# Layer 1's feed-forward: 18 of 22 gate and up tiles as one 2x2 block matrix product with seven block products

## The chip, the cores and the metric

The kernel runs on one core of a Trainium2 chip. The metric is the device time of one execution in microseconds (us). PE is TensorE (matmuls), PEld its weight loads, DVE VectorE, ACT ScalarE, POOL GpSimd, SP the engine whose queue issues the DMAs.

## The reference, cut to what matters

The program is one inference step of a two-layer backbone over 640 tokens (512 of a sample, 128 of a prompt), 1024 channels wide. Each layer has a mixer and then a feed-forward with a hidden width of 2816, all in float32:

```
def _swiglu(h, w_gate, w_up, w_down):
    return (jax.nn.silu(h @ w_gate) * (h @ w_up)) @ w_down
...
        xp = xp + gtf_p * _swiglu(_modulate(_rmsnorm(xp, norm_ffn_g[layer]), shf_p, scf_p), *ffn)
        xs = xs + gtf_s * _swiglu(_modulate(_rmsnorm(xs, norm_ffn_g[layer]), shf_s, scf_s), *ffn)
```

`_rmsnorm` divides each token by its root mean square, `_modulate` is h*(1+scale)+shift with one scale and shift per channel for the sample and one for the prompt. Layer 1's feed-forward is the last stage; a final norm follows.

## The kernel before, in words

Activations lie with channels on the 128 partitions: x is 8 tiles k of 128 channels by T = 640 tokens. Every float32 product is made of three: an operand is split into a rounded high part and the rest (`split`, L185: ACT writes hi at L186, DVE writes lo = x - hi at L187), and hi*hi, hi*lo and lo*hi are accumulated. `gemm` (L280) does this for one tile of 128 output channels: for each k three pairs, each on two halves of the columns, so 48 matmuls for 8 tiles k (L290). The two halves lie in the two banks of one `acc` buffer, of which there are two (pool `mm`); a pool `pm` has four more single banks.

A weight tile comes by one 512 KB DMA on SP's queue into one of two buffers `wraw` (`raw_w`, L269), and is split into one of three buffers `whi` and `wlo` (`split_w`, L274). A tile is loaded as soon as both readers of the older one are done.

`ffn(1)` (L393) works in three parts of 8, 7 and 7 hidden tiles (`FF_PARTS`). For a hidden tile f it loads gate and up weights and runs two `gemm`s on the moving operand `xh`, `xl` with GH = 322 columns to a half: 640 tokens and 4 columns for the shift. The operand is x times the norm's gain, but not yet divided by the root mean square, so that the matmuls can begin ahead of the norm's end; `scaled` (L365) multiplies the result by `rext`, the reciprocal root mean square of each token (DVE, L366). Then come SiLU (ACT, L413), the product with up (DVE, L414) and a split into `hh`, `hl`. After each part the 8 down tiles m run on it (320 columns to a half) and `residual` (L370) adds each into x with three DVE operations (L381). In the last part `ffn_end` (L432) takes the down product in two passes of 384 and 256 columns (L453), adds (L458), squares (L460), and writes the final norm (L470). Its weight tiles m = 3 to 7 are kept in buffers `wd` for the second pass.

The order on each engine is made by a scheduler ahead of time; on the chip each engine runs its list in order and waits at semaphores. The 12 arena buffers (`blk`) and the pools above limit how far it can run ahead.

## Time and profile before

| | |
|---|---|
| three runs of the kernel | 1951.6 us median, 1950.04 to 1951.79 |
| the profiled execution | 1948.95 us |
| its span in the profile | 1947.2 us |
| mean granted TensorE clock | 0.983 of 2.4 GHz |
| PE busy | 1865.1 us |
| DVE busy | 1242.4 us |
| ACT busy | 751.4 us |
| DMA queues' load | 34.4% of 16 engines' span |

The page lists one profiled execution. Busy time is the time in which an engine has an instruction in work; matmuls overlap in the pipeline, so one matmul's duration is longer than the distance to the next, and it is the distance that adds up. Some matmul records can be missing. "Idle before" a row is the time that its engine stood still ahead of it, and the name behind it is what ended that.

### The profile page before, as it was taken

Reading aid. Unit: us, or ns where it says so; the run is one execution under the profiler, and the core shown is the slowest. Engines: PE = TensorE matmul, PEld = TensorE weight load, DVE = VectorE, ACT = ScalarE, POOL = GpSimd, SP = SyncE. Lnnn points to the kernel's source line nnn. Section 1 sums busy time; section 2 is a strip of 40 time slices with the busy share of each in tenths; the row PEclk is TensorE's granted clock in tenths of the full one; section 3 lists DMA queues with packets and bytes.
Section 4 is the critical chain, followed back from the end, with each engine's and each line's share of the span. In section 5 each row is a group of like instructions: output and inputs, shape, how many; then the busy total and the mean of one; then the engine's idle time right before and its main releaser. Section 6 shows DMA issues by size and latency. Waiting matters only on the chain.

```text
span 1947.2 us, 30947 instructions
## 1 busy us (share of the span) xinstructions
PE 1865.1 (96%) x12556; PEld 1738.2 (89%) x12556; DVE 1242.4 (64%) x2041; ACT 751.4 (39%) x1246; POOL 369.4 (19%) x425
## 2 busy tenths in 40 slices
PE   4898999899999999999999999997999999999998
PEld 1886778899999999999988788865999999999997
DVE  7779933668837847876787786969464433433444
ACT  5453344532212212234654665664433221221222
POOL 1038800010000000012034533357341000000002
PEclk8999999999999999999999999999999999999999
DMA  7465355525524534432221222133422222222222
GB/s 289 117 154 175 120 164 129 205 98 174 166 75 150 162 110 148 141 105 89 80 77 55 75 63 92 50 107 92 162 67 76 76 69 75 75 69 84 76 59 83
DMA packets 100991, 215.82 MB, mean 111 GB/s; under 512 B 14944, under 2 KB 50416, under 8 KB 100336
## 3 DMA queue, kind: packets, MB, share of 16 engines
q1 hardware_dynamic: 100816, 213.83, 34.4%
q8 instruction: 99, 1.62, 0.3%
q14 instruction: 44, 0.36, 0.1%
q0 software_dynamic: 32, 0.02, 0.0%
HBM read 192.31 MB, written 18.84 MB: 108 GB/s over the span
## 4 chain that ended last, share of the span: by engine, by line
PE 83%; DVE 3%; ACT 1%; DMA 1%; issue 1%; DVEq 0%; SPq 0%; ACTq 0%
PE acc L290 71%; PE pm L453 1%; PE acc L453 1%; PE pm L627 1%; PE pm L709 1%; PE pm L1094 1%; PE pm L694 1%; DVE ssdw L683 1%; PE acc L1275 1%; PE pm L676 1%; DVE cv L560 1%; DMA ssq<-yd 1%; PE pm L713 1%; PE pm L226 1%; PE pm L1262 0%
## 5 line engine op out<-in xcount | busy, mean ns | idle before, releaser
L290 PE MATMUL acc<-xh,whi 128*128 128x322 f32 (+2 forms) x2320 | 548.3, 316 | 7.2 <-ACT xh L1169 6.2
L290 PE MATMUL acc<-xl,whi 128*128 128x322 f32 (+2 forms) x2320 | 547.8, 315 | 0.0
L290 PE MATMUL acc<-xh,wlo 128*128 128x322 f32 (+2 forms) x2320 | 546.5, 315 | 0.0
L186 ACT ACTIVATE whi<-wraw 128x1024 fp32r<-128x1024 f32 (+2 forms) x212 | 221.1, 1044 | 657.4 <-PE acc L290 416.3
L290 PEld LDWEIGHTS acc<-xh,whi 128*128 128x128 f32 (+1 forms) x2320 | 392.2, 190 | 23.1 <-issue 14.4
L290 PEld LDWEIGHTS acc<-xh,wlo 128*128 128x128 f32 (+1 forms) x2320 | 392.8, 189 | 11.1 <-issue 10.6
L290 PEld LDWEIGHTS acc<-xl,whi 128*128 128x128 f32 (+1 forms) x2320 | 393.6, 189 | 8.4 <-issue 7.9
L182 POOL TENSOR_TENSOR ssq<-ssq 128x640 f32<-128x640 f32 (+2 forms) x45 | 71.6, 1590 | 1122.4 <-ACT ssq L460 453.7
L187 DVE TENSOR_TENSOR wlo<-wraw,whi 128x1024 fp32r<-128x1024 f32 (+2 forms) x212 | 263.3, 1242 | 27.6 <-ACT whi L186 26.5
L366 DVE TENSOR_TENSOR ffw<-acc,rext 128x644 f32<-128x644 f32 x88 | 72.9, 829 | 200.8 <-PE acc L290 197.0
L381 DVE SCALAR_TENSOR_TENSOR x<-acc,mod,x 128x320 f32<-128x320 f32 x144 | 54.5, 434 | 163.9 <-PE acc L290 163.9
L246 DVE CUSTOM_DVE_ANT_0 junk<-adar,cond 128x1024 bf16<-128x1024 f32 x112 | 136.8, 1221 | 1.8
L290 PE MATMUL acc<-hh,wlo 128*128 128x320 f32 x592 | 134.5, 309 | 0.0
L290 PE MATMUL acc<-hl,whi 128*128 128x320 f32 x592 | 134.4, 308 | 0.0
L290 PE MATMUL acc<-hh,whi 128*128 128x320 f32 x592 | 134.2, 309 | 0.0
L560 DVE SCALAR_TENSOR_TENSOR cv<-cv,vecs 128x644 f32<-128x644 f32 x96 | 97.9, 1020 | 15.4 <-ACT cv L558 13.8
L290 PEld LDWEIGHTS acc<-hl,whi 128*128 128x128 f32 x592 | 98.9, 188 | 0.0
L290 PEld LDWEIGHTS acc<-hh,wlo 128*128 128x128 f32 x592 | 98.9, 188 | 0.0
L290 PEld LDWEIGHTS acc<-hh,whi 128*128 128x128 f32 x592 | 98.8, 188 | 0.0
L186 ACT ACTIVATE hh<-ffw 128x640 fp32r<-128x640 f32 x44 | 32.5, 739 | 95.4 <-DVE ffw L414 95.4
L683 DVE SCALAR_TENSOR_TENSOR ssdw<-ssdw,dtk,ssdcb 128x128 f32<-128x128 f32 x160 | 60.5, 442 | 11.3 <-ACT ssdw L681 11.0
L182 POOL TENSOR_TENSOR mt<-s5x,s5co 128x128 f32<-128x128 f32 x79 | 42.8, 550 | 119.4 <-ACT s5x L1034 114.5
(344 smaller groups left out, 2705.4 us busy)
## 6 DMA issues: line engine op xcount, KB each, us to landing
adar<-in_ada_w SPq DMA_DIRECT2D x56, 512.0 KB, 4.2
wraw<-in_ffn_w_gate SPq DMA_DIRECT2D x44, 512.0 KB, 3.3
wraw<-in_ffn_w_up SPq DMA_DIRECT2D x44, 512.0 KB, 3.3
wraw<-in_od_w_in SPq DMA_DIRECT2D x40, 512.0 KB, 3.3
wraw<-in_ffn_w_down SPq DMA_DIRECT2D x32, 448.0 KB, 3.3
wraw<-in_ev_w_in SPq DMA_DIRECT2D x16, 512.0 KB, 4.2
wraw<-in_ffn_w_down SPq DMA_DIRECT2D x16, 512.0 KB, 3.5
wraw<-in_od_w_out SPq DMA_DIRECT2D x16, 512.0 KB, 3.6
```

The lines of the kernel that those rows point to most:

```text
L182: e.tensor_tensor(o, a, b, op=op)
L186: self.nc.scalar.activation(hi, x, AF.Copy)
L187: self.nc.vector.tensor_tensor(lo, x, hi.bitcast(F32), op=OP.subtract)
L226: nc.tensor.matmul(ps[q:q + 32], self.condf[:, 2 * i + a], w[a][:, b * 512:b * 512 + 512], start=i == 0, stop=i == 3)
L246: nc.vector.tensor_tensor_reduce(out=junk, in0=w, in1=self.cond[:, s], scale=1.0, scalar=0.0, op0=OP.mult, op1=OP.add, accum_out=self.mod[ ...
L290: nc.tensor.matmul(ps[:mw, h, :n], a[:, k, :mw], b[:, h * n:(h + 1) * n], start=k0 + k == 0 and q == 0, stop=k0 + k == total - 1 and q == 2)
L366: self.nc.vector.tensor_tensor(t.rearrange("p (h n) -> p h n", h=2), ps[:, :, :GH], self.rext.rearrange("p (h n) -> p h n", h=2), op=OP.mult)
L381: nc.vector.scalar_tensor_tensor(xk[:, a:b], pv, gate[:, m, s:s + 1], xk[:, a:b], op0=OP.mult, op1=OP.add)
L453: nc.tensor.matmul(ps[:, :n], w[:, k], x[:, a:b], start=k == 0 and q == 0, stop=k == nf - 1 and q == 2)
L560: nc.vector.scalar_tensor_tensor(acc, cb[:, k:k + G], cw[:, k * 24 + wi:k * 24 + wi + 1], acc, op0=OP.mult, op1=OP.add)
L627: nc.tensor.matmul(ps, Bt[:, c], xw, start=True, stop=True)
L683: nc.vector.scalar_tensor_tensor(E[:, h], E[:, h], self.dt[:, 0, c, g * 8 + h:g * 8 + h + 1], cbs, op0=OP.mult, op1=OP.mult)
```

## The change

`build` calls `ffn_blocks(1)` instead of `ffn(1)`; layer 0 keeps `ffn`. The hidden tiles now come in parts of 4, 6, 6 and 6.

The first 4 tiles run as before. Beside them `token_forms` makes seven operands out of x: the 1024 channels are cut into two halves of 4 tiles k, the tokens into two halves of 320, and the four blocks b11, b12, b21, b22 (channel half, token half) are normalised, scaled and shifted first. The seven are b11, b21, b22, t1 = b12 - b11, t3 = b22 - b12, t2 = b22 - t1 and t4 = b21 - t2, each split into hi and lo (`fm`, seven arena buffers). One generator step, which makes all seven for one k, follows each of the 4 tiles.

For the other 18 tiles `block_pair` takes gate and up together as a 2x2 block matrix: a and b are the gate tile's two channel halves, c and d the up tile's. DVE makes s1 = c + d, s2 = s1 - a, s3 = a - c, s4 = b - s2 (`fws`). The seven products of 4 tiles k and 320 columns are a*b11, b*b21, s1*t1, s2*t2, s3*t3, s4*b22 and d*t4. Four of them accumulate in one bank X, which is read between them (by ACT for copies, by DVE for sums); one lies in the other bank A of the same `acc` buffer, two in a bank Y of `pm`. Nothing is multiplied by `rext` any more.

```diff
--- before.py
+++ after.py
@@ -428,6 +428,117 @@
                     after[1](m, self.xk(m))
             if last:
                 after[2]()
+
+
+    def token_forms(self, layer, xs):
+        nc = self.nc
+        fm = self.blks("fm", 7, [2, 4, TH], F32R)
+        self.forms = [(t[:, 0], t[:, 1]) for t in fm]
+        sh = self.mod[layer][:, 24:32]
+        for k in range(4):
+            for a, b, d in SEGS:
+                self.tt(nc.vector, xs[:, :, a:b], self.x[:, k::4, a:b], self.rext[:, None, d:d + b - a].to_broadcast([128, 2, b - a]), OP.mult)
+            for i in range(2):
+                for s, (a, b, d) in enumerate(SEGS):
+                    nc.scalar.activation(xs[:, i, a:b], xs[:, i, a:b], AF.Identity, scale=self.amul[:, 4 * i + k, s:s + 1],
+                                         bias=sh[:, 4 * i + k, s:s + 1])
+            b11, b12, b21, b22 = (xs[:, i, h * TH:h * TH + TH] for i in range(2) for h in range(2))
+
+            def put(n, x):
+                self.split(self.forms[n][0][:, k], self.forms[n][1][:, k], x)
+
+            sub = lambda o, x, y: self.tt(nc.vector, o, x, y, OP.subtract)
+            put(0, b11)
+            put(1, b21)
+            put(2, b22)
+            put(4, sub(b11, b12, b11))
+            put(6, sub(b12, b22, b12))
+            put(5, sub(b22, b22, b11))
+            put(3, sub(b21, b21, b22))
+            yield
+
+    def block_pair(self, layer, f, sc, ws, wd):
+        nc = self.nc
+        v = nc.vector
+        rg = self.raw_w(self.I["ffn_w_gate"][layer * NFF + f], 8)
+        ru = self.raw_w(self.I["ffn_w_up"][layer * NFF + f], 8)
+        a, b, c, d = (r[:, i * 4:i * 4 + 4] for r in (rg, ru) for i in range(2))
+        s1, s2, s3, s4 = (ws[:, i] for i in range(4))
+        ab = self.split_w(rg, 8)
+        self.tt(v, s1, c, d, OP.add)
+        self.tt(v, s2, s1, a, OP.subtract)
+        s12 = self.split_w(ws[:, 0:2].rearrange("p i k m -> p (i k) m"), 8)
+        self.tt(v, s3, a, c, OP.subtract)
+        self.tt(v, s4, b, s2, OP.subtract)
+        s34 = self.split_w(ws[:, 2:4].rearrange("p i k m -> p (i k) m"), 8)
+        self.split(wd[:, 0], wd[:, 1], d)
+        acc = self.mm.tile([128, 2, 512], F32, name="acc")
+        X, A, Y = acc[:, 0, :TH], acc[:, 1, :TH], self.psum()[:, :TH]
+
+        def product(ps, w, k0, form, first):
+            xh, xl = self.forms[form]
+            for k in range(4):
+                for q, (m, x) in enumerate(((w[0], xh), (w[0], xl), (w[1], xh))):
+                    nc.tensor.matmul(ps, m[:, k0 + k], x[:, k], start=first and k == 0 and q == 0, stop=k == 3 and q == 2, skip_group_check=not first)
+
+        p1, u2, p5, tu, tg, hd = sc
+        product(X, ab, 0, 0, True)
+        nc.scalar.activation(p1, X, AF.Copy)
+        product(A, ab, 4, 1, True)
+        self.tt(v, tg[:, :TH], A, p1, OP.add)
+        product(X, s12, 4, 5, False)
+        nc.scalar.activation(u2, X, AF.Copy)
+        product(Y, s12, 0, 4, True)
+        nc.scalar.activation(p5, Y, AF.Copy)
+        product(X, s34, 0, 6, False)
+        self.tt(v, tu, X, p5, OP.add)
+        product(Y, s34, 4, 2, False)
+        self.tt(v, tg[:, TH:], Y, u2, OP.add)
+        nc.scalar.activation(tg, tg, AF.Silu)
+        product(X, (wd[:, 0], wd[:, 1]), 0, 3, False)
+        self.tt(v, hd[:, TH:], tu, tg[:, TH:], OP.mult)
+        self.tt(v, hd[:, :TH], X, tg[:, :TH], OP.mult)
+        return hd
+
+    def ffn_blocks(self, layer):
+        nc = self.nc
+        gate = self.mod[layer][:, 40:48]
+        hb = self.big("hb", [2, 4, T], F32R)
+        wk = self.blk("ffw", [BLK])
+        forms = self.token_forms(layer, wk[:, 2 * G:2 * G + 2 * T].rearrange("p (i n) -> p i n", i=2))
+        ht = lambda k: (hb[:, 0, k], hb[:, 1, k])
+        for f0, f1 in ((0, 4), (4, 10), (10, 16), (16, NFF)):
+            nf = f1 - f0
+            if f0 == 4:
+                sb = self.blks("fsc", 2, [BLK])
+                ws = self.blk("fws", [4, 4, 128])
+                wd = self.blk("fwd", [2, 2, 4, 128], F32R)
+                h2 = self.blk("hc", [2, 2, T], F32R)
+                ht = lambda k: (hb[:, 0, k], hb[:, 1, k]) if k < 4 else (h2[:, 0, k - 4], h2[:, 1, k - 4])
+            for f in range(f0, f1):
+                if not f0:
+                    wg = self.load_w(self.I["ffn_w_gate"][layer * NFF + f], 8)
+                    pg = self.gemm(wg, self.xt, 8, GH)
+                    wu = self.load_w(self.I["ffn_w_up"][layer * NFF + f], 8)
+                    pu = self.gemm(wu, self.xt, 8, GH)
+                    tg = self.scaled(wk[:, :G], pg)
+                    hd = self.scaled(wk[:, G:2 * G], pu)
+                    for s, (a, b, d) in enumerate(SEGS):
+                        t, u = tg[:, d:d + b - a], hd[:, d:d + b - a]
+                        nc.scalar.activation(t, t, AF.Silu, bias=tg[:, NS + s:NS + s + 1])
+                        nc.vector.scalar_tensor_tensor(u, u, hd[:, NS + s:NS + s + 1], t, op0=OP.add, op1=OP.mult)
+                        self.split(*(h[:, a:b] for h in ht(f)), u)
+                    next(forms)
+                else:
+                    t = sb[f % 2]
+                    sc = [t[:, i * TH:i * TH + TH] for i in range(4)] + [t[:, 4 * TH:4 * TH + T], t[:, 4 * TH + T:4 * TH + 2 * T]]
+                    self.split(*ht(f - f0), self.block_pair(layer, f, sc, ws, wd[:, f % 2]))
+            if f1 == NFF:
+                self.ffn_end(layer, f0, nf, ht)
+                return
+            for m in range(8):
+                w = self.load_w(self.I["ffn_w_down"][layer * 8 + m][:, f0 * 128:f1 * 128], nf)
+                self.residual(self.xk(m), self.gemm(w, ht, nf, TH), m, gate)
 
     def ffn_end(self, layer, f0, nf, ht):
         nc = self.nc
@@ -1419,7 +1530,7 @@
             K.residual(K.xk(m), ps, m, gate, part[m // 4][:, m % 4])
             K.norm_tile(m, K.xk(m))
         K.norm_end()
-        K.ffn(1)
+        K.ffn_blocks(1)
 
 
 _OUTS = (("y", (128, 8, T)), ("cache", (2, 4, 128, 128)), ("s5", (2, 128, 32)), ("ssd", (2, 4, 128, 512)))
```

The scheduler puts the instructions of neighbouring tiles into one another. Three places show how. All of the program ahead of layer 1's feed-forward has the same order as before.

On DVE, in a tile's turn among the gate and up tiles before, a turn is these seven rows (the next gate's weights, the up product's scaling, the next up's weights, the product with SiLU, the split; `ffw` is the tile's work buffer):

```order
L366 TENSOR_TENSOR ffw_15209<-acc_15105,rext_83 128x644
L187 TENSOR_TENSOR wlo_15276<-wraw_15273,whi_15275 128x1024
L366 TENSOR_TENSOR ffw_15209<-acc_15160,rext_83 128x644
L187 TENSOR_TENSOR wlo_15340<-wraw_15337,whi_15339 128x1024
L414 SCALAR_TENSOR_TENSOR ffw_15209<-ffw_15209 128x512
L414 SCALAR_TENSOR_TENSOR ffw_15209<-ffw_15209 128x128
L187 TENSOR_TENSOR hl0_14978<-ffw_15209,hh0_14976 128x640
```

In the change a turn of a block tile has 14 rows; these are twelve of them, from the third block tile's time (14775 is the fourth tile's gate load, 14777 its up load; `fws` holds s1 to s4, `fsc0` and `fsc1` the scratch of even and odd tiles, `fwd` the split of d):

```order
L182 TENSOR_TENSOR fws_14415<-wraw_14777 128x512
L182 TENSOR_TENSOR fws_14415<-fws_14415,wraw_14775 128x512
L182 TENSOR_TENSOR fsc1_14414<-acc_14559,fsc1_14414 128x320
L182 TENSOR_TENSOR fsc1_14414<-fsc1_14414 128x320
L187 TENSOR_TENSOR wlo_14673<-fws_14415,whi_14672 128x1024
L182 TENSOR_TENSOR fws_14415<-wraw_14775,wraw_14777 128x512
L182 TENSOR_TENSOR fws_14415<-wraw_14775,fws_14415 128x512
L182 TENSOR_TENSOR fsc0_14413<-acc_14678,fsc0_14413 128x320
L187 TENSOR_TENSOR wlo_14780<-wraw_14775,whi_14779 128x1024
L182 TENSOR_TENSOR fsc1_14414<-acc_14559,fsc1_14414 128x320
L187 TENSOR_TENSOR fwd_14416<-wraw_14777,fwd_14416 128x512
L187 TENSOR_TENSOR hb_13556<-fsc1_14414,hb_13556 128x640
```

The turn's other two are the split of s1 and s2 (1024 columns) behind them and a 320-column sum of Y ahead of them. The fourth tile's weights are thus added up and split while the second tile's sums (`fsc1`) are finished.

On PE, in the same turn, at the end of the third block tile's first product (bank X of `acc_14678`), the queue goes on with the two matmuls of the third tile's s1*t1 (`fm4` is t1) in Y (`pm_14679`), and then with the second tile's s3*t3 in its own X (`acc_14559`):

```order
L482 MATMUL acc_14678<-fm0_13678,wlo_14661 128x320
L482 MATMUL pm_14679<-fm4_13682,whi_14666 128x320 x2
L482 MATMUL acc_14559<-fm6_13684,whi_14553 128x320 x2
L482 MATMUL acc_14559<-fm6_13684,wlo_14554 128x320
L482 MATMUL acc_14559<-fm6_13684,whi_14553 128x320 x2
L482 MATMUL acc_14559<-fm6_13684,wlo_14554 128x320
```

Nothing of the kind stood there before, where a tile's 48 matmuls of a product came in a row. In the whole turn the order is: third tile's b11, two matmuls of its t1, second tile's t3, the rest of t1, third tile's b21, second tile's t4, third tile's b22, third tile's t2, and the fourth tile's b11. At no place do two products of the same X follow each other.

On PE, at the seam between the fourth tile and the down tiles, the down tiles m = 0 (`acc_14147`) and m = 1 (`acc_14181`) first run over the hidden tiles 0 to 2, and then both over the hidden tile 3:

```order
L290 MATMUL acc_14181<-hb_13556,whi_14177 128x320 x4
L290 MATMUL acc_14181<-hb_13556,wlo_14178 128x320 x2
L290 MATMUL acc_14147<-hb_13556,whi_14143 128x320
L290 MATMUL acc_14181<-hb_13556,whi_14177 128x320
L290 MATMUL acc_14147<-hb_13556,whi_14143 128x320
L290 MATMUL acc_14181<-hb_13556,whi_14177 128x320
L290 MATMUL acc_14147<-hb_13556,whi_14143 128x320
L290 MATMUL acc_14181<-hb_13556,whi_14177 128x320
L290 MATMUL acc_14147<-hb_13556,whi_14143 128x320
L290 MATMUL acc_14147<-hb_13556,wlo_14144 128x320 x2
L290 MATMUL acc_14181<-hb_13556,whi_14177 128x320
L290 MATMUL acc_14181<-hb_13556,wlo_14178 128x320 x2
```

Before, at its first seam, m = 0 ran over seven of its eight hidden tiles before it needed the eighth.

## Rows read from the trace of the kernel before

**Rows 1.** The page: busy times, and the granted clock in 40 slices (tenths).

```profile
PE 1865.1 (96%) x12556; PEld 1738.2 (89%) x12556; DVE 1242.4 (64%) x2041; ACT 751.4 (39%) x1246; POOL 369.4 (19%) x425
PEclk8999999999999999999999999999999999999999
```

**Rows 2.** Chain that ended last, in order of time: start us, us, what.

```profile
1479.38 406.41 PE acc L290 x2748
```

**Rows 3.** Windows: us, busy by engine (count), PEclk, DMA share, GB/s.

```profile
1495.60:1580.80 85.20, 85.20 (x576) 85.20 (x575) 35.15 (x42) 23.04 (x31) 0.00 (x0) 1.00 0.24 75
1580.80:1637.00 56.20, 56.20 (x386) 56.20 (x385) 19.68 (x33) 9.23 (x10) 0.00 (x0) 1.00 0.24 76
1885.60:1936.50 50.90, 50.76 (x347) 50.26 (x345) 23.48 (x42) 14.66 (x24) 11.67 (x12) 1.00 0.22 68
1936.50:1947.20 10.70, 1.29 (x7) 0.81 (x6) 4.42 (x12) 0.68 (x2) 0.00 (x0) 0.61 0.29 99
```

**Rows 4.** Timeline of layer 1's feed-forward: start us, us, engine, line, operation, count.

```profile
1566.81 0.83 DVE L366 TENSOR_TENSOR ffw<-acc,rext 128x644 f32<-128x644 f32 x1 [5.05 <-PE acc L290]
...
1580.85 0.45 PE L290 MATMUL acc<-hh,whi 128*128 128x320 f32 x2
...
1581.05 0.83 DVE L366 TENSOR_TENSOR ffw<-acc,rext 128x644 f32<-128x644 f32 x1 [5.04 <-PE acc L290]
...
1585.54 0.45 PE L290 MATMUL acc<-hl,whi 128*128 128x320 f32 x2
...
1888.78 0.34 PE L453 MATMUL pm<-hh,whi 128*128 128x384 f32 x1
...
1891.76 0.34 PE L453 MATMUL pm<-hh,wlo 128*128 128x384 f32 x1
```

**Rows 5.** Groups by form from 1479.4 us on: count | busy, mean ns of one | idle before.

```profile
L187 DVE TENSOR_TENSOR wlo<-wraw,whi 128x1024 fp32r<-128x1024 f32 x48 | 58.7, 1223 | 0.9 <-ACT whi L186 0.3
L186 ACT ACTIVATE whi<-wraw 128x1024 fp32r<-128x1024 f32 x48 | 51.0, 1062 | 209.9 <-PE acc L290 124.0 <-issue 85.1 <-ACT rext L360 0.9
L366 DVE TENSOR_TENSOR ffw<-acc,rext 128x644 f32<-128x644 f32 x44 | 36.5, 829 | 165.5 <-PE acc L290 163.4 <-ACT rext L360 2.2
L187 DVE TENSOR_TENSOR hl<-ffw,hh 128x640 fp32r<-128x640 f32 x22 | 18.2, 826 | 17.7 <-ACT hh L186 17.7
L414 DVE SCALAR_TENSOR_TENSOR ffw<-ffw 128x512 f32<-128x512 f32 x22 | 16.4, 746 | 0.8 <-ACT ffw L413 0.8
L186 ACT ACTIVATE hh<-ffw 128x640 fp32r<-128x640 f32 x22 | 16.3, 739 | 46.8 <-DVE ffw L414 46.8
L414 DVE SCALAR_TENSOR_TENSOR ffw<-ffw 128x128 f32<-128x128 f32 x22 | 7.6, 346 | 0.0
L182 DVE TENSOR_TENSOR ssq<-ssq 128x384 f32<-128x384 f32 x1 | 0.6, 558 | 0.7 <-ACT ssq L460 0.7
L357 ACT ACTIVATE rext<-pm 128x512 f32<-128x512 f32 x1 | 0.6, 600 | 2.6 <-PE pm L356 2.6
L360 ACT ACTIVATE rext<-pm 128x128 f32<-128x128 f32 x1 | 0.3, 271 | 0.0
L290 PEld LDWEIGHTS acc<-hh,wlo 128*128 128x128 f32 x240 | 40.1, 188 | 0.0
```

**Rows 6.** Timeline of DVE: operations that follow each other without a wait.

```profile
1568.80 1.01 DVE L414 SCALAR_TENSOR_TENSOR ffw<-ffw 128x512 f32<-128x512 f32 x2
...
1602.14 1.14 DVE L381 SCALAR_TENSOR_TENSOR x<-acc,mod,x 128x320 f32<-128x320 f32 x3 [4.76 <-PE acc L290]
```

**Rows 7.** Timeline of DVE at the stage's start.

```profile
1480.10 0.83 DVE L366 TENSOR_TENSOR ffw<-acc,rext 128x644 f32<-128x644 f32 x1 [2.18 <-ACT rext L360]
```

**Rows 8.** DMA issues: count, KB each, median us from issue to landing.

```profile
adar<-in_ada_w SPq DMA_DIRECT2D x56, 512.0 KB, 4.2
wraw<-in_ffn_w_gate SPq DMA_DIRECT2D x44, 512.0 KB, 3.3
wglu<-in_s_w_glu SPq DMA_DIRECT2D x1, 1024.0 KB, 6.4
```

## The prediction

> **What bounds the kernel now.** The page comes first: PE is busy for 96% of the span, DVE for 64%, ACT for 39%, and the granted clock stands at nine tenths or more (2.4 GHz) from the second slice on [rows 1]. A share is an average, so the chain of waits comes next. There the changed stage is one piece: from 1479.38 us PE runs `gemm` after `gemm` for 406.41 us without another engine on the path [rows 2]. The windows say the same of its parts: among gate and up tiles and among down tiles PE has work for the whole window at a granted clock of 1.00, DVE for 41 and 35% of it [rows 3]. So here a matmul less is time less, as long as DVE, ACT and the weight loads keep up.
>
> **What a matmul costs.** From the scaling of one tile's up product (1566.81) to that of the next tile's (1581.05) lie 14.24 us and 96 matmuls of 322 columns [rows 4]: 148 ns each, 14.24 us a tile. From 1580.85 to 1585.54 there are 16 rows of two matmuls of 320 columns: 4.69/32 = 147 ns. In `gemm` two banks take turns; a block product puts 12 matmuls in a row into one bank. `ffn_end` does that too: 17 steps of 384 columns from 1888.78 to 1891.76 take 175 ns each [rows 4], by columns 146 ns for 320. One bank costs nothing extra; I take 146.6.
>
> **Removed and added on PE.** A block tile has 7 x 4 x 3 = 84 matmuls of 320 columns: 84 x 0.1466 = 12.31 us for 14.24, so 1.93 us less, 18 times 34.7 us. (By 146 ns it would be 35.4.) The down products keep their columns; 4, 6, 6 and 6 tiles make the same sum as 8, 7 and 7. The last 10.70 us stay [rows 3]. The page "TensorE: Matmul & The Clock Gate" of the Trainium skill, section "Back-to-back issue gap", gives N/2.4 + 2.5 ns between single matmuls. By it a tile would take 13.12 and a block tile 11.41 us, and the gain would be 30.8 us; the rows show 11 ns more per matmul, so the measured steps decide.
>
> **Added on DVE, block tiles.** Sizes that the trace lacks are read between neighbours: 512 columns 0.69 and 320 columns 0.49 us, from 384 at 0.558 and 640 at 0.826. A block tile has three splits of 1024 (1.223), one of 640 (0.826), four weight sums and one split of 512, five operations of 320: 3.67 + 0.83 + 3.46 + 2.46 = 10.4 us [rows 5]. Operations that adjoin take less than their durations add up to: 512 and 128 columns take 1.01 together, 1.09 apart [rows 6], so about 9.3 at best. ACT has three of 1.062, one of 0.6, three of 320 columns from PSUM (0.44, between 0.271 and 0.600) and two of 0.739: 6.6 us [rows 5]. Both lie below 12.31, but DVE now is 76 to 85% full, so its order counts.
>
> I walked one turn of the block stage by hand, in the order that the scheduler made, with these durations and 0.2 us from a product's last step to its reader (the next product starts at 1580.85, the scaling at 1581.05 [rows 4]). With PE never stopping, each wait ends in time. The tightest is the copy of X after s2*t2: ACT first splits s1 and s2 of the next tile, and ends 0.35 us before PE adds s3*t3. Next are DVE's read of X ahead of d*t4 (2 us to spare) and the free `acc` for the tile after (about 2 us). I allow 0.5 us for all 18 tiles; both ends are 0 and 0.35 for each, 6 us.
>
> **The weight loads.** There are two `wraw` for a gate and an up load, so up's next load starts only after DVE's split of d. From its landing to the next such split DVE has five operations of 512, four of 320 and two of 1024: 3.46 + 1.96 + 2.45 = 7.87 us. With 3.3 us from issue to landing [rows 8] the ring takes 11.2 us, and 12.1 with 4.2, the median beside other traffic: under 12.31, and hidden. SP's queue carries the same number of gate and up loads, and 32 instead of 24 down loads of fewer columns, in order.
>
> **Added in the first four tiles.** `token_forms` adds to DVE, per tile, two products with `rext` (1.23 and 0.42), four differences and seven splits of 320 (5.4): 13.2 us with the tile's own work, 11.5 when they adjoin, against 14.24 of PE. ACT gets four modulations and seven copies, some 5 us. PE's gate and up products need only that DVE scales each one in 7 us, which holds. But DVE starts at 1480.10, when the norm is done [rows 7], with PE already 13 us into the stage, and DVE's list has the fourth tile's forms ahead of its split.
>
> **The seams.** This is where I expect losses; before there were almost none.
> - Fourth tile to down. PE can run m = 0 and 1 over hidden tiles 0 to 2, 36 matmuls, 5.3 us. From the end of the up product DVE must scale it and do three splits of forms, a weight split, three differences and the product with SiLU before the hidden tile is split: with 0.2 us ahead 5.9 when they adjoin, and some 10 if DVE comes late to it. So 0.6 to 4.7 us; I take 1.5, nearer to the short one, because DVE has gaps to catch up. Then m = 0 and 1 end together and hold both `acc`, so m = 2 waits for `residual`, 1.14 us [rows 6]: 1.0.
> - Down to the first block tile. Both loads of the second block tile go out together, after s4 at 0.5 us, and land by 5.2 (4.7 lies between 3.3 for one load and 6.4 for 1024 KB [rows 8]); 4.6 us of DVE follow until its first weights are split, 9.8, where PE has come at 9.1: 0.7 (0 to 1.4). At the two later seams 0.4 in all.
> - Last block tile to down, twice: the down tile m = 1 needs the `acc` from which DVE still takes the last product: 0.2 + 0.49 us, then 0.3 for `residual`. 2.0 in all.
> - Into `ffn_end`: the same 0.7, and ACT squares m = 0 before it splits the weights of m = 3: 1.8. PE stood still for almost nothing there before [rows 3]. 2.5.
>
> The sum: -34.7 + 0.5 + 2.5 + 1.1 + 2.0 + 2.5 = -26.1 us. The profiled execution took 1948.95, so 1922.9; the median of the runs is 2.65 above it, and I predict **1925 us**. With no seam lost it would be 1951.6 - 34.7 = 1917; with each seam at its upper end (5.7 + 2 + 3 + 3.5) and 6 in the tiles some 1937. That is this case's own range, 1915 to 1937.
>
> **The rivals.**
> - *DVE becomes the bound* of the block tiles. For it: 76 to 85% busy, and DVE waits for ACT before each split; the split of a hidden tile waits 17.7/22 = 0.80 us today [rows 5]. Against it: the order puts other operations between ACT's half and DVE's. Were four of the five splits to wait 0.80, a turn would take 10.4 + 3.2 = 13.6, 18 x 1.3 = 23 us more: 1948. No change, or half of that.
> - *The weight ring is too slow*, and the kernel slower than before. If the gate and up loads hold each other up, as one transfer of 1024 KB at 6.4 us [rows 8], the ring takes 14.3, 18 x 2.0 = 35 us more: 1960. It begins to bind at 4.4 us from issue to landing and eats the gain at 5.9. Against it: the two go out over a microsecond apart, and the DMA engines are a quarter busy [rows 3].
> - *The bank X stops PE.* Were PE to wait at each of X's three returns until the reader is done, 2 x (0.2 + 0.44) + 0.2 + 0.49 = 2.0 us a tile and 35 in all would cancel the gain: 1961, slower. It decides if the product ahead of a return is X's own. The Trainium skill speaks against this part of the change: "Perfetto Trace Analysis", section "Matmuls", wants independent groups to rotate through banks so that the reading of one overlaps the next group. The built order sets other banks' products between, so I hold it unlikely; no row of before has such a return.
> - *A product costs more than its columns*: if a weight load (188 ns [rows 5]) were no longer hidden behind its matmul's neighbours and set the step, 84 x 0.188 = 15.8 us a tile, 63 us more: 1988. The single-bank rows at 175 ns speak against it.
>
> **How the numbers follow.** About 0.2%, 3.9 us, can be told from no change. The forecast's own case has 0.75. DVE as the bound 0.12, of which 0.08 still faster and 0.04 the same; the weight ring 0.07, of which 0.01 the same; the bank 0.04; dear products 0.02. Faster 0.83, same 0.05, slower 0.12. The range must leave out no more than 2 in 10: it goes from 1915 up to 1946, which takes in most of the DVE case and leaves out the three slow ones and the ends.
>
> **What would show it.** Right: in a window over the block tiles PE has work throughout, 12.3 us from one tile's first product to the next's; DVE is 75 to 85% busy; the product rows have steps of 146 to 147 ns; idle time of PE stands only at the four seams, 8 us in all, with `residual`, the hidden split and the weights `wd` as releasers. Wrong: a turn of 13 us or more, with PE waiting for a split (DVE is the bound), with DVE waiting for `wraw` (the ring), or for the copies of X; or PE waiting inside the first four tiles.

## The result and the profile after

The changed kernel takes **1921.95 us** (four runs, 1921.51 to 1923.59) where the kernel before took 1951.41 beside it: a ratio of 0.9852 (0.9835 to 0.9869), 29.5 us less. Predicted were 1925 us, 1915 to 1946. The profiled execution took 1922.12 us; the sum of the prediction, made against the profiled execution of before, gave 1922.9.

The page, to be held against [rows 1]: PE is as full as before with fewer matmuls, DVE goes from 64 to 70%.

```profile
PE 1837.2 (96%) x12340; PEld 1710.7 (89%) x12340; DVE 1342.8 (70%) x2255; ACT 818.7 (43%) x1374; POOL 369.6 (19%) x425
PEclk8899999999999999999999999999899999999999
```

Windows of the changed kernel, each over two turns of block tiles, one pair from each of the three parts (us, busy of PE, PEld, DVE, ACT, POOL with counts, PEclk, DMA share, GB/s; the counts take in instructions that a window's edges cut):

```profile
1581.58:1606.19 24.61, 24.61 (x170) 24.61 (x170) 19.60 (x29) 13.00 (x18) 0.00 (x0) 1.00 0.27 86
1699.04:1723.65 24.61, 24.61 (x170) 24.61 (x170) 18.57 (x27) 12.77 (x18) 0.00 (x0) 1.00 0.28 86
1816.35:1840.97 24.62, 24.62 (x171) 24.62 (x170) 19.54 (x29) 13.00 (x18) 0.00 (x0) 1.00 0.26 87
```

A turn is 12.305 us, 168 matmuls of 146.5 ns in two, at a granted clock of 1.00 (2.4 GHz), and PE has work for all of it. DVE is busy for 9.6 us of a turn and ACT for 6.5, on the average of the three windows. The tile before took 14.24 [rows 4].

PE's waits from the stage's start on, in the list by releaser (us in total, times, longest):

```profile
PE pm L344 <- DVE ssq L182: 1.8, 1, 1.8
PE pm L564 <- ACT wd L186: 1.3, 1, 1.3
PE acc L290 <- DVE fsc L182: 1.2, 2, 0.6
PE acc L290 <- DVE ffw L366: 0.9, 1, 0.9
PE acc L290 <- DVE x L381: 0.9, 1, 0.9
PE acc L564 <- DVE fsc L182: 0.7, 1, 0.7
PE pm L577 <- DVE rs L348: 0.6, 1, 0.6
```

The first and the last belong to the norm at the end and were there before (1.7 and 0.6, all that the same list of before has). No wait has a block product (L482) behind it: all stand at seams. A list counts only the idle time; what a seam costs is read in the timeline, as the distance between starts less the steps of 146.5 ns (148 for 322 columns, 175 for 384). PE at the start of the stage, at the third down tile, from a part's last block tile to the down tiles (the first of two such places), and at two places in `ffn_end`:

```profile
1481.63 0.46 PE L290 MATMUL acc<-xh,wlo 128*128 128x322 f32 x2
1482.98 0.54 PE L290 MATMUL acc<-xh,whi 128*128 128x322 f32 x2 [0.90 <-DVE ffw L366]
...
1532.54 0.46 PE L290 MATMUL acc<-hb,wlo 128*128 128x320 f32 x2
1533.87 0.38 PE L290 MATMUL acc<-hb,whi 128*128 128x320 f32 x1 [0.88 <-DVE x L381]
...
1631.53 1.92 PE L482 MATMUL acc<-fm,fwd 128*128 128x320 f32 x12
1634.03 0.86 PE L290 MATMUL acc<-hb,whi 128*128 128x320 f32 x4 [0.58 <-DVE fsc L182]
...
1867.12 1.93 PE L482 MATMUL acc<-fm,fwd 128*128 128x320 f32 x12
1869.73 0.59 PE L564 MATMUL acc<-hb,whi 128*128 128x384 f32 x2 [0.68 <-DVE fsc L182]
...
1873.83 0.34 PE L564 MATMUL acc<-hc,wlo 128*128 128x384 f32 x1
1875.47 0.62 PE L564 MATMUL pm<-hb,wd 128*128 128x384 f32 x2 [1.30 <-ACT wd L186]
```

Start of the stage 1.05 us; third down tile 1.04; last block tile to down 0.74, and 0.31 for `residual` at 1640.61, twice in all, 2.1; into `ffn_end` 0.85 + 1.47 and 0.5 lost in the next few steps, 2.8. That is 7.0 us; before the same places cost 0.3. So 34.7 - 6.7 = 28.0 us should be gone from the stage, and from its first matmul to the end of the span it went from 482.1 to 454.3 us, 27.8 less: the stage is accounted for to 0.2 us. The profiled executions differ by 26.8 us, because the stage began 0.9 us later in this one (1466.0 for 1465.1), with the same order ahead of it. The traces below, none with an edit ahead of the stage, begin it between 1464.3 and 1469.8, so that is no effect of the change. The medians differ by 29.5, because the median of before lies 2.5 us above its profiled execution and that of the change at its own.

The first wait is one that the prediction did not have. DVE at the stage's start, where [rows 7] had the scaling at once:

```profile
1480.87 1.23 DVE L182 TENSOR_TENSOR ffw<-x,rext 128x1024 f32<-128x1024 f32 x1 [2.01 <-ACT rext L357]
1482.02 0.82 DVE L366 TENSOR_TENSOR ffw<-acc,rext 128x644 f32<-128x644 f32 x1
```

`token_forms`' first product, x times `rext`, goes ahead of the scaling that frees `acc`.

### The profile page after: what moved, and what is told of

The parts are those of the page before. It is cut to its first block, busy times and chain, and to the rows that moved or that the text cites. A ratio compares the mean times of both kernels' runs of the same rounds, so it can differ in the third digit from the quotient of the medians.

```text
span 1920.3 us, 30941 instructions
## 1 busy us (share of the span) xinstructions
PE 1837.2 (96%) x12340; PEld 1710.7 (89%) x12340; DVE 1342.8 (70%) x2255; ACT 818.7 (43%) x1374; POOL 369.6 (19%) x425
## 4 chain that ended last, share of the span: by engine, by line
PE 82%; DVE 4%; ACT 1%; issue 1%; DMA 1%; DVEq 0%; SPq 0%; ACTq 0%
PE acc L290 59%; PE acc L482 8%; PE pm L482 3%; PE acc L564 1%; PE pm L738 1%; PE pm L564 1%; PE pm L820 1%; DVE ssdw L794 1%; PE pm L1205 1%; PE pm L805 1%; PE pm L787 1%; DVE cv L671 1%; PE acc L1386 1%; PE pm L824 1%; PE pm L226 1%
## 5 line engine op out<-in xcount | busy, mean ns | idle before, releaser
L290 PE MATMUL acc<-xh,whi 128*128 128x322 f32 (+1 forms) x1744 | 417.7, 319 | 8.4 <-ACT xh L1280 6.2
L290 PE MATMUL acc<-xl,whi 128*128 128x322 f32 (+1 forms) x1744 | 416.5, 317 | 0.0
L290 PE MATMUL acc<-xh,wlo 128*128 128x322 f32 (+1 forms) x1744 | 415.9, 317 | 0.0
L186 ACT ACTIVATE whi<-wraw 128x1024 fp32r<-128x1024 f32 (+3 forms) x202 | 204.0, 1011 | 489.1 <-PE acc L290 322.3
L290 PEld LDWEIGHTS acc<-xh,whi 128*128 128x128 f32 x1744 | 296.4, 190 | 24.6 <-issue 14.3
L290 PEld LDWEIGHTS acc<-xh,wlo 128*128 128x128 f32 x1744 | 296.2, 190 | 11.1 <-issue 10.6
L290 PEld LDWEIGHTS acc<-xl,whi 128*128 128x128 f32 x1744 | 297.5, 190 | 8.4 <-issue 7.9
L187 DVE TENSOR_TENSOR wlo<-wraw,whi 128x1024 fp32r<-128x1024 f32 (+3 forms) x202 | 242.6, 1202 | 33.0 <-ACT whi L186 32.5
L482 PE MATMUL acc<-fm,whi 128*128 128x320 f32 x576 | 127.5, 309 | 0.0
L482 PEld LDWEIGHTS acc<-fm,whi 128*128 128x128 f32 x576 | 96.2, 188 | 0.1
L482 PE MATMUL acc<-fm,wlo 128*128 128x320 f32 x288 | 88.8, 309 | 0.0
L794 DVE SCALAR_TENSOR_TENSOR ssdw<-ssdw,dtk,ssdcb 128x128 f32<-128x128 f32 x160 | 60.4, 441 | 11.2 <-ACT ssdw L792 11.0
```

The lines of the kernel that those rows point to most:

```text
L186: self.nc.scalar.activation(hi, x, AF.Copy)
L187: self.nc.vector.tensor_tensor(lo, x, hi.bitcast(F32), op=OP.subtract)
L290: nc.tensor.matmul(ps[:mw, h, :n], a[:, k, :mw], b[:, h * n:(h + 1) * n], start=k0 + k == 0 and q == 0, stop=k0 + k == total - 1 and q == 2)
L482: nc.tensor.matmul(ps, m[:, k0 + k], x[:, k], start=first and k == 0 and q == 0, stop=k == 3 and q == 2, skip_group_check=not first)
L794: nc.vector.scalar_tensor_tensor(E[:, h], E[:, h], self.dt[:, 0, c, g * 8 + h:g * 8 + h + 1], cbs, op0=OP.mult, op1=OP.mult)
```

## The experiments

The theory: PE bounds the block tiles at 12.31 us a turn, DVE and the loads are hidden, and the rest of the 34.7 us is lost at the seams. The rivals: the gain comes from something else in the change; or DVE, the weight ring (the two `wraw` buffers, loaded and used in turn) or the bank X is nearer to the bound than it looks. Ratios are to the kernel before, run on the same chip; "over the changed kernel" is the difference of ratios times 1951.6. A sharper measure is "the stage" in each profiled execution, from the stage's first matmul to the end of the span: the two traces of the changed kernel differ by 0.2 us in it. The section ends with a table of it.

**What the other parts of the change do.**

```diff
-        for f0, f1 in FF_PARTS:
+        for f0, f1 in parts:
...
-        K.ffn(1)
+        K.ffn(1, parts=((0, 4), (4, 10), (10, 16), (16, 22)))
```

> The kernel before, with layer 1's 22 hidden tiles in parts of 4, 6, 6 and 6 instead of 8, 7 and 7, and nothing else of the change. If the whole gain comes from the 84 matmuls that stand for 96, the parts alone gain nothing: PE has the same 2112 + 768 + 288 matmuls by columns, and the time is that of before, 1950 to 1954 us (a seam more, at most about 2 us). Rival: the parts themselves bring some of the gain (an earlier first down product, a shorter last part), then 1945 or less.

Measured: 1.0014 (1.0004 to 1.0023), 2.7 us slower. Its list of waits has two that before did not have:

```profile
PE pm L453 <- ACT wd L186: 0.9, 1, 0.9
PE acc L290 <- DVE x L381: 0.7, 1, 0.7
```

With forms, buffers and parts, and plain tiles throughout (beyond the lines shown, the later tiles use `fsc` as scratch and number their hidden tiles from the part's start):

```diff
-                if not f0:
+                if True:
...
-                    next(forms)
+                    if not f0: next(forms)
```

> The change with its parts, its seven operands and their buffers, but with plain gate and up products for all 22 tiles: the operands are made beside the first four tiles and not used. It prices what the change adds outside the block tiles. In the changed kernel PE stood still for 1.1 us at the start of the stage (the first operand's product with rext goes ahead of the scaling that frees acc) and 1.1 us at the third down tile, so 1 to 3 us over the parts alone, some 1953 to 1955. Rival: making the operands costs more, because DVE then has 13.2 us of work for 14.24 of PE: 1958 or more, with PE waiting inside the first four tiles.

Measured: 1.0014 (1.0004 to 1.0023) again. The list has 0.9 us for `ffw` at the start and 0.9 for the third down tile, but 0.4 for `wd`, and nothing inside the first four tiles: the forms cost little more than the wait at the start, 1.1 us of stage over parts_alone. From this kernel to the changed one the ratio falls by 0.0162, 31.6 us (30.4 of stage), and only the 18 later tiles differ. The rival that the parts or the forms bring the gain falls: the block products bring all of it and pay for their seams.

**What bounds a turn next.** The last product of every block tile, d*t4, is left out:

```diff
-        product(X, (wd[:, 0], wd[:, 1]), 0, 3, False)
+        pass
```

> Each block tile leaves out its last product, d*t4 (the sum X is read without it); all the work of DVE, ACT and the loads stays. It asks what bounds a turn next, after PE. PE's turn is then 72 x 0.1465 = 10.55 us. If nothing else is near, 18 x 1.76 = 31.7 us less than the changed kernel: 1890. If DVE is next (10.4 us of single operations), about the same, 1890 to 1893. If the weight ring is next, the turn stops at the ring's own time: in the changed kernel's trace one went from an up load's issue at 1586.62 over its use to the next issue at 1598.68, 12.06 us, and if that is its shortest, the gain is 18 x 0.25 = 5 us: 1917; at the 11.2 us of the prediction it is 1902.

Measured: 0.9707 (0.9690 to 0.9724), 28.3 us under the changed kernel of 31.7. A product of 12 matmuls is worth nine tenths of its time, 1.57 us of 1.76. Most of the missing 3 us is inside the tiles now: in the list PE waits for ACT's copy of Y. SP's timeline has the up loads 11.6 and 12.6 us apart where PE's turn would be 10.55, and the chain of work that ended last shows how that reaches PE, from the load over ACT's splits to the product in Y:

```profile
PE pm L482 <- ACT fsc L492: 3.1, 10, 0.5
```

```profile
1576.15 1.06 SPq L271 DMA_DIRECT2D wraw<-in_ffn_w_up  x1
...
1588.78 0.33 SPq L271 DMA_DIRECT2D wraw<-in_ffn_w_up  x1
...
1600.38 0.33 SPq L271 DMA_DIRECT2D wraw<-in_ffn_w_up  x1
```

```profile
1588.78 4.14 DMA wraw<-in_ffn_w_up
1593.48 1.04 ACT whi L186
1594.53 0.74 ACT hb L186
1595.65 2.03 PE pm L482 x12
```

So the ring is next after PE, as the prediction's 11.2 to 12.1 said. Eighteen turns longer by 1.05 us would have lost 19; the up loads at the start of a part go out only 8.1 to 8.9 us apart, and I put it down to this lead that most of it is hidden over six tiles.

**How much DVE has left.** Four, and eight, more operations a tile that nobody reads:

```diff
-        self.tt(v, tu, X, p5, OP.add)
+        self.tt(v, tu, X, p5, OP.add); [self.tt(v, p1, tu, p5, OP.add) for _ in range(4)]
```

> Each block tile gets four more additions of 320 columns on DVE whose result nobody reads (0.49 us each alone, about 0.40 adjoining). If only DVE's sum of work counts, 10.4 + 1.6 to 2.0 = 12.0 to 12.4 us, 11 when operations adjoin, is still hidden under PE's 12.31: 1921 to 1924. If the weight ring has no slack, what stands between an up load's landing and the split of d grows by three of them or so, 1.2 to 1.5 us: 18 x 1.2 = 22 us more, less what the lead of one tile covers at the start of each part: 1935 to 1945.

> Eight more additions of 320 columns on DVE in each block tile instead of four. In a window of 49 us (four turns) DVE was busy 38.84 us in the changed kernel and 43.65 with four more, 1.2 us a turn for four; with eight a turn has 9.75 + 2.4 = 12.15 us of DVE, just under PE's 12.31. If the sum alone counts, still 1921 to 1926. If DVE cannot do without its waits for the up load and for ACT (1.3 us a turn with four more), a turn takes some 13.3 us and 18 turns 18 us more, less the lead at the start of each part: 1932 to 1942, with PE waiting for wlo or fsc.

Measured: 0.9858 (0.9843 to 0.9874) with four, no change; 0.9878 (0.9854 to 0.9902) with eight, 5 us over the changed kernel. Its interval reaches into the changed kernel's, but its stage is 5.1 us longer too. The same window of 49 us (four turns) in the changed kernel, with four and with eight, one kernel to a fence:

```profile
1567.00:1616.00 49.00, 49.00 (x337) 49.00 (x336) 38.84 (x56) 26.06 (x37) 0.00 (x0) 1.00 0.26 81
```

```profile
1567.00:1616.00 49.00, 49.00 (x336) 49.00 (x335) 43.65 (x72) 25.58 (x37) 0.00 (x0) 1.00 0.22 74
```

```profile
1567.00:1616.00 49.00, 48.41 (x326) 47.56 (x326) 47.67 (x85) 24.39 (x35) 0.00 (x0) 1.00 0.24 80
```

With eight, DVE (the third busy time) is at 97% and sets the pace: d*t4 begins at 1594.18 and 1606.79, 12.61 us a turn for 12.31, and PE waits for it inside the block tiles:

```profile
PE acc L482 <- DVE fsc L182: 1.9, 5, 0.5
```

So almost all of DVE's idle time in the changed kernel, some 2.5 us a turn, is spare, and not a chain of waits that it needs. The DVE rival was further off than its chance of 0.12 made it.

**The bank X.** First each tile's products in the order of the code, which keeps the scheduler from setting two tiles into each other:

```diff
-            xh, xl = self.forms[form]
+            xh, xl = self.forms[form]; es = ExitStack(); es.enter_context(self.behind(nc.tensor))
...
+            es.close()
```

> PE takes a block tile's seven products in the order of the code, one tile after the other, instead of the scheduler's mixture of two tiles. Between two products of the same bank X then stands one product of another bank, 1.76 us. The reader of X needs 0.2 + 0.44 us (ACT copy) or 0.2 + 0.49 (DVE sum), so it ends in time unless its engine is in a long split (1.06 on ACT: 0.2 + 1.06 + 0.44 = 1.70). If one product between two returns is enough, no change against the changed kernel: 1920 to 1925 us. If the mixture of two tiles is what hides the readers, PE waits 0.3 to 1 us at several of the returns of each tile: 1930 or more.

> As tiles_in_order, but with s2*t2 directly behind a*b11, so that once in a tile X is written again with no other product between. The wait is then at least 0.2 + 0.44 us for the copy p1, and up to 1.7 where ACT is in a split: 18 x 0.64 = 11.5 us to 18 x 1.7 = 31 us over tiles_in_order, so 1933 to 1955. If returns to a bank cost nothing on PE (the copy is overlapped anyway), 1920 to 1925.

Measured: **1.0037** (1.0026 to 1.0048) in order, 36 us over the changed kernel, the whole gain and more; 0.9988 (0.9978 to 0.9997) with t2 directly behind a*b11, 27 us over it. Of the first expectation the slow case came, that the mixture hides the readers, but not at the places where it looked for the waits. The second failed in its sign: x_adjacent was to be 11.5 to 31 us slower than tiles_in_order and is 10 us faster; that its time lies in the range given for it is chance. The list of the first names two waits a tile:

```profile
PE acc L482 <- DVE fsc L182: 14.3, 18, 1.9
PE acc L482 <- ACT fsc L486: 12.3, 18, 0.7
```

and the timeline shows where they stand: between a*b11 and b*b21, and between b*b21 and s2*t2.

```profile
1587.71 0.31 PE L482 MATMUL acc<-fm,wlo 128*128 128x320 f32 x1
1588.73 0.56 PE L482 MATMUL acc<-fm,whi 128*128 128x320 f32 x2 [0.70 <-ACT fsc L486]
...
1590.45 0.31 PE L482 MATMUL acc<-fm,wlo 128*128 128x320 f32 x1
1591.41 0.56 PE L482 MATMUL acc<-fm,whi 128*128 128x320 f32 x2 [0.65 <-DVE fsc L182]
```

At 1588.73 the product of b21 begins, in bank A, and what it waited for is the copy of bank X. No data make it wait; X and A are the two banks of one `acc` buffer. If the waits go by the buffer, they end when A lies anywhere else; the order of the code stays as in tiles_in_order:

```diff
-        X, A, Y = acc[:, 0, :TH], acc[:, 1, :TH], self.psum()[:, :TH]
+        X, A, Y = acc[:, 0, :TH], self.psum()[:, :TH], self.psum()[:, :TH]
```

> As tiles_in_order, but the product b*b21 goes to a bank of pm instead of the second bank of X's acc buffer. In tiles_in_order PE waited for the copy p1 before that product, though it writes another bank, and for the sum that reads A before X was written again: 26.6 us by releaser, 36 us in the time. If PE's waits go by the whole acc buffer, taking A out of it ends both, because between two returns of X stands a product of 1.76 us and its reader needs 0.64 to 0.69: 1922 to 1928 us. If what counts is that only one product stands between the returns, the waits stay, at X's second and third return, and the time stays at 1945 or more.

Measured: 0.9844 (0.9828 to 0.9860), as fast as the changed kernel. Of the waits of a block product the list keeps one:

```profile
PE acc L482 <- ACT fsc L486: 0.4, 1, 0.4
```

In x_adjacent, too, the buffer was at work: there s2*t2, directly behind a*b11, waits for the first copy, p1 (L486), and b*b21 in bank A for the second, u2 (L488). Neither waits for DVE's sum, and the two waits add up to 19.5 us instead of 26.6, most of the difference between the two runs:

```profile
PE acc L482 <- ACT fsc L486: 10.0, 18, 0.7
PE acc L482 <- ACT fsc L488: 9.5, 18, 0.5
```

So one other product of 1.76 us between two returns of X is enough, and the 26.6 us of waits in tiles_in_order came from the shared buffer. In the changed kernel the same products share the buffer, and the mixture of two tiles hides the waits. In the stage in_order_a_apart is even 2.7 us shorter than the changed kernel; its list has none of the three waits for `fsc` at the seams. That the bank rival's price was met (35 us predicted, 36 measured) is luck: it counted three waits a tile, each ahead of a product in X for X's own reader, 0.64 to 0.69 us, and two others came, one ahead of A for X's reader and one ahead of X for A's. One of its steps is confirmed by x_adjacent: where the product ahead of a return is X's own, PE waits, 0.56 us each for 0.64.

**The weight ring.** Each up load waits for a load of half of it into the same buffer:

```diff
-        self.nc.sync.dma_start(raw[:, :nk, :mw], ...)
+        [self.nc.sync.dma_start(raw[:, :n, :mw], ...[:, :n]) for n in ([nk // 2] if more else []) + [nk]]
...
-        ru = self.raw_w(self.I["ffn_w_up"][layer * NFF + f], 8)
+        ru = self.raw_w(self.I["ffn_w_up"][layer * NFF + f], 8, more=True)
```

> Each up load of a block tile is preceded by a load of half of it into the same buffer, which it must wait for: from issue to landing some 2.5 us more than the 4.4 us of the changed kernel, about 6.9. It prices the rival of the weight ring. With six products the ring turned in 11.5 us with loads of 4.1 us, so it is 7.4 us and the load: 14.3 us a turn, 2.0 us over PE's 12.31, 18 x 2.0 = 36 us less the lead at the start of each of three parts (two turns' worth, some 4 us each): 1940 to 1950. If there is slack that the ring does not show, because DVE and ACT take the operations in another order when a load is late, under 1930.

Measured: 0.9917 (0.9902 to 0.9932), 13 us over the changed kernel, between the two cases expected. The chain of waits, from the first part (start us, us, what), follows the ring:

```profile
1577.10 2.58 DMA wraw<-in_ffn_w_up
1579.69 3.23 DMA wraw<-in_ffn_w_up
...
1589.14 3.32 DMA wraw<-in_ffn_w_up
1592.47 4.00 DMA wraw<-in_ffn_w_up
...
1602.76 3.42 DMA wraw<-in_ffn_w_up
```

The two loads together take 5.8 and 7.3 us; from the landing (1582.92, 1596.47) to the next issue DVE needs 6.2 and 6.3 us (6.7 to 7.1 in the later turns of the other two parts), not the 7.87 of the prediction nor the 7.4 of the expectation, because the scheduler sets nine operations there instead of the changed kernel's eleven. Turns of 12.0 and 13.6 follow, and of the rival's price a good third. In this order the ring would bind at 12.31 - 6.25 = 6.1 us from issue to landing in the first part, and at 5.2 to 5.6 in the others, rather than at 4.4. In the changed kernel's own order the eleven operations are those that the prediction counted: an up load that landed at 1578.8 is followed by the next issue at 1586.62, 7.8 us later. Its loads in the stretch from 1567 to 1616 us are at the limit of 4.4 already, without a wait of PE:

```profile
wraw<-in_ffn_w_up SPq DMA_DIRECT2D x3, 512.0 KB, 4.4
```

So the run prices a longer load in an order of its own. How much longer a load the changed kernel's order would bear is not shown.

**The seams mended.** One mend for each kind of wait: the first operands behind the first tile's scalings on DVE; the weights `wd` split ahead of the first square; odd down tiles in two banks of `pm` (`Two` puts two such banks in place of an `acc`).

```diff
+                    up = [i for i in nc.cur_bb.bb.instructions if i.engine == nc.vector.engine][-1]
...
-                    next(forms)
+                    with self.tc.issue_after(up):
+                        next(forms)
...
-                self.residual(self.xk(m), self.gemm(w, ht, nf, TH), m, gate)
+                ps = Two((self.psum(), self.psum())) if m % 2 else None
+                self.residual(self.xk(m), self.gemm(w, ht, nf, TH, ps=ps), m, gate)
...
-                if len(ws) == m:
+                while len(ws) < min(m + 5, 8):
...
-                nc.scalar.activation(sq if m else ssq, x, AF.Square)
+                with self.behind(nc.scalar):
+                    nc.scalar.activation(sq if m else ssq, x, AF.Square)
```

> The changed kernel with three mends, one for each kind of wait that its trace shows on PE. (1) The first operand's product with rext stands behind the first tile's two scalings on DVE: 1.1 us at the start. (2) In the last part ACT and DVE split the weights of the down tiles 3 and 4 ahead of the first square: 1.8 us, and the rest of that seam may go too. (3) Odd down tiles accumulate in two banks of pm instead of acc, so a down tile needs no acc that residual or the last block tile still holds: 1.1 + 2 x 1.0 us. If these seams are what the kernel lost against 34.7 us, PE's waits at them vanish and the time is 4 to 6 us under the changed kernel: 1916 to 1918 against 1951.6, a ratio near 0.982. If something else comes late behind each (the hidden split behind the third down tile, a weight load in the last part), 1919 to 1922.

Measured: 0.9842 (0.9821 to 0.9863), a median of 1920.28 us; its span, 1915.5 us, was 4.8 under the changed kernel's, but the ratios could not be told apart. So both were run side by side:

> The changed kernel once more, beside the mended one on the same chip, so that the two can be told apart: a ratio of 0.985 to before, as in its first timing (0.9835 to 0.9869).

> The kernel with the three mended seams once more, in more rounds. In its first profile PE's waits from the stage's start on fell from 7.4 to 3.0 us (what is left is in the final norm and 0.6 at the seams) and its span was 4.8 us shorter than that of the changed kernel, while the ratios of the times overlapped. If those waits are time, this kernel is 4 to 5 us, 0.2 to 0.25%, faster than the changed one beside it. If the saving is given back elsewhere, the two are within 1 us.

Measured: the changed kernel 0.9855 (0.9831 to 0.9879), 1921.77 us (1920.15 to 1927.73); the mended one 0.9818 (0.9803 to 0.9832), **1915.55 us** (1915.11 to 1917.01). The runs do not overlap; the intervals of the ratios still touch. What is left of PE's waits ahead of the final norm:

```profile
PE acc L295 <- DVE x L386: 0.3, 1, 0.3
PE pm L295 <- DVE wlo L192: 0.3, 1, 0.3
```

The seams were time: 6.2 us between the medians side by side, and 6.2 to 6.8 of stage (two traces of each kernel) for the 7.0 read at the seams. The list shows nothing else that came late in their place. The first timing alone, with its ratio 0.0010 under the changed kernel's, would have said 2. Against before the gain is 31 and 35.5 us in the two timings and 34.2 to 34.6 of stage, and PE's matmuls are worth 34.7.

The stage in every trace:

| run | stage, us | against the changed kernel |
|---|---|---|
| before | 482.1 | +27.8 |
| changed kernel, and once more (changed_again) | 454.3, 454.1 | |
| parts_alone | 483.6 | +29.3 |
| forms_alone | 484.7 | +30.4 |
| six_products | 426.5 | -27.8 |
| dve_plus4 | 454.2 | -0.1 |
| dve_plus8 | 459.4 | +5.1 |
| tiles_in_order | 487.5 | +33.2 |
| x_adjacent | 479.5 | +25.2 |
| in_order_a_apart | 451.6 | -2.7 |
| up_load_longer | 466.9 | +12.6 |
| seams_mended, seams_again | 447.5, 447.9 | -6.8, -6.4 |

## Why the prediction was right

By its steps, in its order:

- *The block tile on PE*, 84 matmuls at 146.6 ns for 12.31 us: 12.305 measured, in all three parts. The page "TensorE: Matmul & The Clock Gate" of the Trainium skill, section "Back-to-back issue gap", has a formula for the isolated matmul; by it, as an estimate, a step is 135.8 ns and the block tile 11.41 us. The rows disagree with that by 11 ns a step, as those of before did.
- *DVE's and ACT's steps.* The sizes read between neighbours hold: 512 columns 0.686 to 0.689 (0.69), 320 columns 0.486 to 0.492 (0.49), ACT's copies from PSUM 0.420 to 0.438 (0.44); ACT's split of 512 is 0.631 (0.6). A turn of DVE is 9.6 us (9.3 to 10.4), of ACT 6.5 (6.6).

```profile
L182 DVE TENSOR_TENSOR fsc<-acc,fsc 128x320 f32<-128x320 f32 x54 | 26.3, 487 | 26.9 <-PE acc L482 26.9
L187 DVE TENSOR_TENSOR fwd<-wraw,fwd 128x512 fp32r<-128x512 f32 x17 | 11.7, 686 | 0.1
L486 ACT ACTIVATE fsc<-acc 128x320 f32<-128x320 f32 x18 | 7.9, 436 | 6.3 <-PE acc L482 5.8
```

- *Waits inside the block tiles*, 0.5 us allowed: none. The walk through one turn by hand gave the right answer, and tiles_in_order shows that it was the order that had to be walked. What it walked were the readers of each bank; that a product also waits for the reader of the other bank of its buffer was not in it, and the built order hid that as well.
- *The weight ring*, 11.2 to 12.1 us: hidden, and 11.6 when six products pressed it. DVE's term was right (7.8 for 7.87), the load's was short: 4.4 us in the block tiles for 3.3 to 4.2, which by the prediction's own sum leaves nothing to spare. What a longer load would cost was overrated: 13 us, where the rival's arithmetic had over 30, though the scheduler had a new order for it.
- *The first four tiles.* "PE's gate and up products need only that DVE scales each one in 7 us": true of the tiles, but **the start was missed**. The step sent DVE to the scaling at 1480.10 because before it did so; in the built order `token_forms`' product of 1.23 us stands ahead. 1.05 us.
- *Fourth tile to down*: 1.5 for the hidden split, measured 0 (DVE came to it early, as in the short case; it ended at 1531.6, 5.6 us after DVE began to scale the up product, and PE did not stop for it), and 1.0 for the third down tile, measured 1.04.
- *Down to block tiles*: 1.1 in all, measured 0 at all three places.
- *Last block tile to down*: 2.0, measured 2.1. *Into `ffn_end`*: 2.5, measured 2.8, with the two causes it named.

The seams sum to 8.6 in the prediction, with the 0.5 inside the tiles, and to 7.0 in the trace: 3.1 us that were allowed for did not come (0.5, 1.5 and 1.1), 1.05 came that was not seen, and the others were 0.4 larger. So the mechanism was right, PE by its matmuls less the seams, but the closeness of the sum (1922.9 for 1922.12) is in part luck: misses of either sign offset each other, and of the 1.7 us that the stage fell further than forecast, the later start took back 0.9. Most of the 3 us between 1925 and the median of 1921.95 is the 2.65 that was added because the profiled execution of before was a quick one; the changed kernel's lay at its median.

Of the rivals the bank was the one to fear: the section "Matmuls" of "Perfetto Trace Analysis" in the Trainium skill wants independent groups to rotate through banks, so that the reading of one overlaps the next. in_order_a_apart agrees: one product of 1.76 us in another buffer between two returns leaves 0.4 us of waits in 18 tiles. tiles_in_order shows that it was not enough here: it rotates through as many banks, and lost 36 us because two of them shared a buffer.

## What to carry to other kernels

Where PE has work throughout and the others have room, count matmuls: 12 fewer of 320 columns are 1.76 us, of which six_products kept nine tenths even with the weight ring's turn already the longer one. Then look for the loss at the places where one kind of tile follows another, engine by engine, the first operation of a new helper among them. Before an accumulator is used again and again within a tile, see what is set between its returns, and whether two banks share one buffer, because the program's waits may go by the buffer.

## What was not expected

- A wait on the other bank of a buffer: PE stood for 0.7 us ahead of a product in bank A for a copy out of bank X, 18 times, and no longer when A was a buffer of its own.
- DVE, one of three engines that hand work to each other within a turn, could be filled to 97% of a window in which PE was busy for 99%.
- A stop of PE costs more than its listed idle time. In tiles_in_order a turn is 14.20 us (d*t4 at 1584.34 and 1598.54) for 12.31, 1.89 more, where the list has 0.70 and 0.65: 0.27 us for each stop on top. The rows above show where: idle time is counted from the end of the last matmul, 0.31 us after its start, where in a stream the next would have started after 0.15; and the two matmuls behind a stop take 0.56 us instead of 0.46.
